# A ring of attention keys gets a copy of its first unit behind its end

## The chip, the cores and the metric

The kernel runs on one core of a Trainium2 chip. The metric is the device time of one execution in microseconds (us); a lower time is better. The profile is of one execution, recorded by the hardware profiler.

## What is computed

One encoder layer over 4096 tokens of 1024 channels. Two head groups run side by side: windowed attention (8 query heads of 64 channels, 2 key/value heads, each query sees keys at most 128 tokens away) and a pooling group. The part that the change touches is the product of queries and keys. Cut down, the reference says:

```python
kw = jnp.concatenate([kp[:, :-2], kp[:, 1:-1], kp[:, 2:]], axis=2)   # 3 blocks of 128 keys
s = jnp.einsum('bnqkgd,bnskd->bnkgqs', qb, kw).astype(jnp.float32) * scale
s = jnp.where(valid[None, :, None, None], s + bias[None, None], NEG)
m = jnp.maximum(jnp.max(s, axis=-1, keepdims=True), sk)
p = jnp.exp(s - m)
p = p / (jnp.sum(p, axis=-1, keepdims=True) + jnp.exp(sk - m))
o = jnp.einsum('bnkgqs,bnskd->bnqkgd', p.astype(v.dtype), vw)
```

Here `n` is a block of 128 queries; its keys are the block before, the block itself and the block behind it.

## The kernel before

The kernel has two stages. The first one, until some 500 us, norms the input, multiplies it by the gate and pooling weights and leaves what the second stage reads in DRAM. The second stage does the attention, the output projection and the closing norm. It walks over units of 256 tokens (two blocks each), from the first token to the last; units and blocks are numbered backwards in the code, and `ru(u)` and `rb(b)` turn a number into its place in the order of the tokens. "Block 7" below is the place in the order of the tokens.

Numbers are kept as pairs of float16 (a high part and a rest), so that every product is three products: high by high, rest by high, high by rest. The keys of a unit are projected by `proj_k` into PSUM, from which ScalarE writes the high part (`keep_k`) and VectorE the rest (`rest_k`) into `k_all`. That tile holds 2 x 1024 columns (high and rest): a ring of four units, in which a unit's place is its token number modulo 1024. Keys of both key heads lie in it, one in the upper and one in the lower 64 partitions.

`scores` is one visit of a block for half of its query heads. For the inner blocks it works in four parts of 32 queries, each against the 288 keys that these can see, for two heads in the two halves of the array at once (`gg`) and two PSUM tiles (`jj`): 2 x 3 x 4 x 2 = 48 matmuls of 32 x 288. The first two blocks and the last one take 128 queries at once, 12 matmuls. Where a part's 288 keys go over the end of the ring, the loop over `(lo, cut, k0), (cut, hi, 0)` makes two matmuls of it, one up to the ring's end and one from its beginning. That is the case for all four parts of blocks 7, 8, 15, 16, 23 and 24.

After a visit comes its softmax: VectorE adds the bias and takes the maximum (`logits`), ScalarE does the exponentials, VectorE and ScalarE make the probabilities as float16 pairs (`probs`, `rests`), and SP issues a transposing DMA into `pt_all` (`turn`). `values` multiplies them by the values of the unit later on.

The order on every engine is written out by hand: each step is put on a list by `due` with a planned time, `pe` and `visit` advance the plan's clock for TensorE, `settled` moves some steps on the other engines out of the softmax's way, and in the end the list is sorted by time and issued under a manual schedule. A plan time thus sets an order only; how long something takes is up to the engines. One turn of the loop over `m` covers two units (four blocks, eight visits). In it lie also three kinds of matmuls that the prediction names by their code: `q_product` (the queries of four units by a scheme with few products, from slots that `load_x` fills; "p3" reads the slot "Z"), `do_kv` (keys and values of a unit), and `product` (the output projection; its inputs are made by `high` on ScalarE and `low` on GpSimd). GpSimd also multiplies by the closing norm's gain (`gain`) and issues the DMAs of `add_x`. SP issues all other loads, stores and transposes in one queue.

Of the kernel before, what the change touches and what calls it, by code (L numbers as in the profile page):

```python
# [9 lines left out]
F16 = mybir.dt.float16  # L10
# [7 lines left out]
P = 128  # L18
# [33 lines left out]
UT = 2 * P  # L52
# [19 lines left out]
def hybrid_layer(ctx: ExitStack, tc, io, out):  # L72
    nc = tc.nc
# [81 lines left out]
    with ExitStack() as actx:  # L155
# [25 lines left out]
        def due(t, fn, *args):  # L181
            plan.append((t, len(plan), fn, args))
# [141 lines left out]
        gg = pa.tile([P, KT, P], BF16, name="gg", tag="yt")  # L324
# [861 lines left out]
        def tile0(si, t):  # L1186
            due(t, mm, si)
            after0(si, t + SLOT)
            return t + SLOT
# [10 lines left out]
        t = tile0(1, 29.3)  # L1200
# [8 lines left out]
        t = tile0(3, t + 1.9)  # L1209
# [9 lines left out]
        t = tile0(8, t + 4.2)  # L1219
# [4 lines left out]
        t = tile0(10, t)  # L1224
        t_last(1, t + 1.5)
        t = tile0(9, t)
# [6 lines left out]
        t = tile0(11, t)  # L1233
# [3 lines left out]
        t = tile0(4, t)  # L1237
        pair_split(5, t - 0.1)
        t = tile0(6, t)
        t_first(9, t + 5.5)  # L1240
        t_last(9, t + 10.0)
        t = tile0(5, t)
# [152 lines left out]
        for m in range(1, NM):  # L1395
# [7 lines left out]
            def op_at(i, z=z, step=step):  # L1403
                return z + i * step
# [13 lines left out]
            for i in range(7):  # L1418
                for c, q in enumerate(quads):
                    t = op_at(i) + c * PT  # L1420
# [8 lines left out]
    pb1 = ctx.enter_context(tc.tile_pool(name="pb1", bufs=1, reuse_waits="tile"))  # L1429
# [8 lines left out]
    wo[O12] = wo[OT4]  # L1438

    RK = 4 * UT  # L1440
    k_all = pb1.tile([P, 2, RK], F16, name="k_all")
    wq_b = pb1.tile([P, 3, 2, 2, HK, P], F16, name="wq_b")
    p_all = pb1.tile([P, 4, 3 * P], F32, name="p_all")
    q_t, v_t = {}, {}


    def rb(b):
        return NB - 1 - b

    def ru(u):  # L1450
        return NU - 1 - u
# [31 lines left out]
    def split_l(dst_h, dst_l, acc):  # L1483
        nc.vector.scalar_tensor_tensor(
            out=dst_l, in0=acc, scalar=QKV_EVAC, in1=dst_h, op0=ALU.mult, op1=ALU.subtract
        )
# [14 lines left out]
    def keys(b):  # L1501
        return [kb for kb in range(3) if 0 <= rb(b) - 1 + kb < NB]
# [10 lines left out]
    s_bank = [ps_s.tile([P, 2, 512], F32, name=f"s{i}") for i in range(2)]  # L1513

    def scores(b, half):
        u, tl = b // 2, rb(b) % 2 * P
        kbs = keys(b)
        first = (rb(b) - 1 + kbs[0]) * P
        if 0 < b < NB - 2:
            parts = [(QR * r, QR, QR * r, QR * r + NK) for r in range(P // QR)]  # L1520
        else:
            parts = [(0, P, 0, len(kbs) * P)]
        s_t[b, half] = s_bank
        for jj in range(2):
            for n, (qi, ki) in enumerate(((0, 0), (1, 0), (0, 1))):
                for r0, nr, lo, hi in parts:
                    k0 = (first + lo) % RK
                    cut = min(hi, lo + RK - k0)
                    for c0, c1, kc in ((lo, cut, k0), (cut, hi, 0)):
                        for gg in range(2 * (c1 > c0)):  # L1530
                            a = slice(64 * gg, 64 * gg + 64)
                            nc.tensor.matmul(  # L1532
                                s_bank[jj][r0 : r0 + nr, gg, c0:c1],
                                q_t[u, half][a, qi, jj, tl + r0 : tl + r0 + nr],
                                k_all[a, ki, kc : kc + c1 - c0], start=(n == 0 and c0 == lo),
                                stop=(n == 2 and c1 == hi), skip_group_check=True,
                            )

    def logits(b, half, i):

# [182 lines left out]
    def k_part(u, i):  # L1723
        ts = slice(ru(u) * UT % RK, ru(u) * UT % RK + UT)
        return k_all[:, i, ts]
# [6 lines left out]

    def rest_k(u):
        split_l(k_part(u, 0), k_part(u, 1), kv_t[u][:, 0])

    def keep_v(u):
        v_t[u] = pb.tile([P, 2, 2, P], F16, name=f"vv{u}", tag="v", bufs=3)
        split_h(v_t[u][:, 0], v_acc(u))
# [365 lines left out]
    def pe(us, fn, *args):  # L2104

        due(now[0], fn, *args)
        now[0] += us
        return now[0]
# [4 lines left out]
    def visit(b, half):  # L2113
        now[0] = max(now[0], free[0])
        t = max(pe(1.1, scores, b, half), free[1])
        softmax(b, half, t)
        free[:] = t + 2.9, t + 7.9

    def do_kv(u, i=2, late=0.0, k_high=0.0, k_low=0.5):
        pe(2.6, proj_k, u, i)  # L2120
        t = pe(2.8, proj_v, u)
        due(t - 2.8 + late + k_high, keep_k, u)
        due(t - 2.8 + late + k_low, rest_k, u)
        due(t + late, keep_v, u)
        due(t + 0.5 + late, rest_v, u)

# [75 lines left out]
    u = NU - 1  # L2202
# [8 lines left out]
    do_q(u, 0, 2)  # L2211
    due(now[0] - 2.0, lambda: nc.scalar.activation(dummy, mhalf, AF.Exp))
    do_kv(u, 0, 0.0, 0.2, 0.8)

    visit(NB - 1, 0)
    do_q(u, 1, 1)
    due(pe(2.6, q_product, 1, "p1", 0), q_keep, 1)
    due(now[0], load_x, 1, "Y")
    visit(NB - 1, 1)
    do_kv(u - 1, 2, 0.0, 0.7, 1.9)  # L2220
    visit(NB - 2, 0)
    turn_22(u, now[0] + 5.0)
# [7 lines left out]
    due(now[0], load_wq, 7, 2)  # L2230
    due(now[0] + 0.1, load_x, 1, "Z")
    do_kv(u - 2, 2)

    for m in range(1, NM):
# [25 lines left out]
        t = pe(M, q_product, m, "p2", 0, "p1")  # L2260
# [37 lines left out]
        t = pe(M, q_product, m, "p7", 1)  # L2298
# [10 lines left out]
        t = pe(M, q_product, m, "p4", 1, "p7")  # L2309
# [44 lines left out]
    at_(2.6, open_second, 2)  # L2354
    at_(2.6, product, 2, "s1", OT1, 1)
    at_(5.2, scores, 1, 0)
    at_(6.3, product, 1, "11", O11, 0)
    at_(8.9, product, 2, "s4", O22, 1, True)
    at_(11.5, values, 2)
    at_(13.6, scores, 1, 1)  # L2360
    at_(14.7, product, 1, "22", OT4, 2)
    at_(17.3, product, 1, "12", O21, 0, True)
# [161 lines left out]
```

## Time and profile before

| | |
|---|---|
| times of three runs | 1168.46, 1169.52, 1170.8 us (median 1169.52) |
| span of the profiled execution | 1163.3 us, first to last instruction (its own total time is not on the page) |
| TensorE busy (matmuls) | 1128.0 us, 97% |
| VectorE / ScalarE / GpSimd busy | 924.2 us, 79% / 758.0 us, 65% / 283.8 us, 24% |
| matmuls | 12528, of which 3432 score products |
| granted TensorE clock | 0.997 |
| DMA moved | 265.00 MB, mean 228 GB/s |

PE stands for TensorE, DVE for VectorE, ACT for ScalarE, POOL for GpSimd, SP and SPq for the SyncE queue that issues DMAs. In the timeline a row is: start, duration of the whole group, engine, line of the code, operation, what it writes and reads, shape, how many; in brackets the time that the engine idled before it and what ended that. In the table by stretches a row is: from and to, length, then busy time and number of instructions of PE, of PE's weight loads, of DVE, ACT and POOL, then granted clock, DMA share and GB/s. Matmuls overlap each other, so a step's cost on PE is read from its start to the start of the next step rather than from the duration of a row.

### The profile page before, as it was taken

How to read it: one execution, taken by the hardware profiler on the slowest of the kernel's cores; microseconds unless marked ns; L12 is line 12 of the kernel's file. 1: busy time of each engine (PE TensorE's matmuls, PEld its weight loads, DVE VectorE, ACT ScalarE, POOL GpSimd, SP SyncE). 2: the span in 40 equal slices, each digit the busy share in tenths (PEclk: the TensorE clock that was granted, in tenths of full speed). 3: DMA queues.
4: the chain of work that ended last, by engine and by line, in shares of the span. 5: the costliest groups of instructions: out<-in, count | busy, mean ns of one | idle time of the engine just before them, and what ended most of it. 6: DMA issues, size and time to landing. Idle time of an engine off the chain costs nothing.

```text
span 1163.3 us, 30484 instructions
## 1 busy us (share of the span) xinstructions
PE 1128.0 (97%) x12528; PEld 833.6 (72%) x12528; DVE 924.2 (79%) x1910; ACT 758.0 (65%) x1696; POOL 283.8 (24%) x270
## 2 busy tenths in 40 slices
PE   5999999999999999999999999999999999999997
PEld 4548888888888888887576676667666666766643
DVE  5788887778878886957887878878778778778896
ACT  5756666676465635166687767777677776777673
POOL 1000000000000000001454444454354444544322
PEclk9999999999999999999999999999999999999999
DMA  9577898696989856989799989899799899899877
GB/s 265 149 237 271 211 259 286 260 310 219 305 244 264 276 198 173 344 285 259 196 191 214 211 213 212 183 235 211 157 228 216 189 219 207 201 222 212 176 187 217
DMA packets 312635, 265.00 MB, mean 228 GB/s; under 512 B 214528, under 2 KB 275584, under 8 KB 303792
## 3 DMA queue, kind: packets, MB, share of 16 engines
q1 hardware_dynamic: 308464, 248.38, 78.1%
q0 software_dynamic: 4032, 14.68, 7.4%
q8 instruction: 98, 1.61, 0.5%
q14 instruction: 41, 0.34, 0.1%
HBM read 132.97 MB, written 79.21 MB: 182 GB/s over the span
## 4 chain that ended last, share of the span: by engine, by line
PE 45%; DVE 3%; DMA 3%; ACT 1%; issue 1%; SPq 0%; DVEq 0%; POOLq 0%; ACTq 0%
PE ms L2017 11%; PE aq_p L1754 9%; PE m L2017 8%; PE s L1532 4%; PE kv L1493 3%; PE kv L1716 3%; PE o L1870 3%; DMA pt_all<-pn 2%; PE z L1989 1%; PE o L1847 1%; DMA xt<-x_scr 1%; DVE pn L1605 1%; DVE p_all L1550 1%; PE ob L1847 1%; PE s L1989 0%
## 5 line engine op out<-in xcount | busy, mean ns | idle before, releaser
L990 PEld LDWEIGHTS <-wa 128*128 128x128 f16 x3360 | 329.7, 98 | 43.5 <-issue 4.8
L990 PE MATMUL ch<-xt,wa 128*128 128x256 f16 x1920 | 214.5, 274 | 2.6 <-ACT cbig L1002 1.7
L1561 ACT ACTIVATE p_all<-p_all,nm 128x384 f32<-128x384 f32 (+1 forms) x256 | 152.4, 596 | 41.3 <-DVE nm L1550 41.3
L1605 DVE SCALAR_TENSOR_TENSOR pn<-p_all,rd,pn 128x384 f16<-128x384 f32 (+1 forms) x256 | 144.5, 624 | 36.9 <-ACT pn L1597 36.1
L2017 PE MATMUL ms<-wo,ys 128*128 128x512 f16 x720 | 165.4, 379 | 2.9 <-DVE ys L1923 0.9
L1597 ACT ACTIVATE pn<-p_all,rd 128x384 f16<-128x384 f32 (+1 forms) x256 | 134.7, 597 | 36.6 <-DVE rd L1583 17.6
L1550 DVE CUSTOM_DVE_ANT_0 p_all<-s,ybig,nsink 128x384 f32<-128x384 f32 (+1 forms) x256 | 155.6, 663 | 1.7 <-PE s L1532 1.7
L2017 PEld LDWEIGHTS <-ys 128*128 128x128 f16 x720 | 68.8, 98 | 83.9 <-issue 2.5
L2017 PE MATMUL m<-wo,y 128*128 128x512 f16 x540 | 124.0, 379 | 1.4 <-DVE mo L2059 1.3
L990 PE MATMUL cl<-xt,wa 128*128 128x256 f16 x960 | 106.7, 273 | 0.8 <-DVE cbig L1015 0.6
L1923 POOL TENSOR_TENSOR y<-yf,y 128x512 f16<-128x512 f32 x29 | 33.5, 1157 | 270.4 <-DMA wo<-w_scr 158.9
L2017 PEld LDWEIGHTS <-y 128*128 128x128 f16 x540 | 51.6, 98 | 62.4 <-issue 2.5
L1754 PEld LDWEIGHTS <-raw 128*128 128x128 f16 x864 | 83.3, 98 | 18.0 <-issue 5.4
L211 POOL TENSOR_SCALAR ssq<-ssq 128x4 f32<-128x4 f32 (+1 forms) x11 | 3.6, 325 | 348.5 <-ACT jk L202 342.7
L1754 PE MATMUL aq_p<-xt,raw 128*128 128x256 f16 x672 | 77.9, 273 | 1.1 <-DVE nm L1550 1.1
L303 DVE TENSOR_TENSOR xt<-ybig,xt 128x1024 f16<-128x1024 f32 x56 | 67.2, 1219 | 13.0 <-ACT xt L298 11.4
L1923 POOL TENSOR_TENSOR ys<-at,ys 128x512 f16<-128x512 f32 x28 | 33.8, 1205 | 147.5 <-ACT ys L1919 123.9
L1532 PE MATMUL s<-k_all,q 64*32 64x288 f16 (+7 forms) x3432 | 63.1, 265 | 1.5 <-ACT k_all L1481 0.9
L1024 ACT ACTIVATE gp<-cbig,cg 128x256 f32<-128x256 f32 x42 | 19.0, 499 | 67.8 <-DVE cbig L1015 64.6
L2054 POOL TENSOR_TENSOR mo<-mo,ybig 128x512 f32<-128x512 f32 x39 | 51.4, 1317 | 44.2 <-ACT jkb L2043 43.9
L298 ACT CAST xt<-ybig 128x1024 f16<-128x1024 f32 x56 | 57.1, 1040 | 4.0 <-PE cl L990 2.1
L1754 PE MATMUL aq_p<-xt,wq_b 128*128 128x256 f16 x504 | 58.6, 273 | 0.0
(211 smaller groups left out, 1948.7 us busy)
## 6 DMA issues: line engine op xcount, KB each, us to landing
x_scr<-xt SPq DMA_DIRECT2D x16, 1024.0 KB
xt<-x_scr SPq DMA_DIRECT2D x16, 1024.0 KB
xn<-in_x SPq DMA_DIRECT2D x28, 512.0 KB
ybig<-in_xT SPq DMA_DIRECT2D x28, 512.0 KB
y_scr<-xt SPq DMA_DIRECT2D x14, 1024.0 KB
xt<-y_scr SPq DMA_DIRECT2D x14, 1024.0 KB
mo<-in_x POOLq DMA_DIRECT2D x28, 512.0 KB, 7.5
out<-mo SPq DMA_DIRECT2D x28, 512.0 KB
```

The costliest lines, as they stand in the source:

```text
L298: nc.scalar.copy(couple(m, c)[:, w, 0], y_view(i))
L303: eng.tensor_tensor(out=o[:, w, 1], in0=y_view(i), in1=o[:, w, 0], op=ALU.subtract)
L990: nc.tensor.matmul(acc[:, c], wa[:, q, wi, slot * HK + k, c * P : (c + 1) * P], x[:, xi, k, :], start=(fresh and n == 0), stop=(n > 3 * 2 ...
L1532: nc.tensor.matmul(s_bank[jj][r0 : r0 + nr, gg, c0:c1], q_t[u, half][a, qi, jj, tl + r0 : tl + r0 + nr], k_all[a, ki, kc : kc + c1 - c0], ...
L1550: nc.vector.tensor_tensor_reduce(out=p_t[b, half][:, hh, :nk], in0=s_t[b, half][jj][:, gg, :nk], in1=bias[:, h, lo : lo + nk], scale=negc[ ...
L1561: nc.scalar.activation(p[:, hh, :nk], p[:, hh, :nk], AF.Exp, bias=nm_t[b, half][:, hh : hh + 1], scale=-1.0, accum_out=den_t[b, half][:, h ...
L1597: nc.scalar.activation(prob_view(b, half)[:, 0, i], p_t[b, half][:, i, :nk], AF.Copy, scale=rd_t[b, half][:, 0, i : i + 1],)
L1605: nc.vector.scalar_tensor_tensor(out=pn4[:, 1, i], in0=p_t[b, half][:, i, :nk], scalar=rd_t[b, half][:, 0, i : i + 1], in1=pn4[:, 0, i], o ...
L1754: nc.tensor.matmul(acc[:, jj], w[:, wi, jj, k, :], x[:, xi, k, :], start=(first and n == 0), stop=(last and n > 3 * 2 * HK - 3), skip_grou ...
L1923: eng.tensor_tensor(out=y[:, :, 1], in0=f(u), in1=y[:, :, 0], op=ALU.subtract)
L2017: nc.tensor.matmul(z_t[u, tag], y[:, k, yi, :], wo[o][:, wi, k, :], start=(n == 0 and acc is None), stop=(n == 3 * HK - 1), skip_group_che ...
L2054: eng.tensor_tensor(out=mo, in0=mo, in1=gpost[:, cs], op=ALU.mult)
```

## The change

The tile of keys gets 256 columns more, behind the ring's end. When the keys of a unit are written that stands at the ring's first place (`ru(u) * UT % RK == 0`, from the second time on: the units at 1024, 2048 and 3072 tokens), GpSimd copies its high part and rest into these columns (`again_k`, 128 x 2 x 256 float16). `scores` then reads the keys of a part as one piece, which may run into the copy.

```diff
-    k_all = pb1.tile([P, 2, RK], F16, name="k_all")
+    k_all = pb1.tile([P, 2, RK + UT], F16, name="k_all")
...
-                    k0 = (first + lo) % RK
-                    cut = min(hi, lo + RK - k0)
-                    for c0, c1, kc in ((lo, cut, k0), (cut, hi, 0)):
-                        for gg in range(2 * (c1 > c0)):
-                            a = slice(64 * gg, 64 * gg + 64)
-                            nc.tensor.matmul(
-                                s_bank[jj][r0 : r0 + nr, gg, c0:c1],
-                                q_t[u, half][a, qi, jj, tl + r0 : tl + r0 + nr],
-                                k_all[a, ki, kc : kc + c1 - c0], start=(n == 0 and c0 == lo),
-                                stop=(n == 2 and c1 == hi), skip_group_check=True,
-                            )
+                    k0 = first % RK + lo
+                    for gg in range(2):
+                        a = slice(64 * gg, 64 * gg + 64)
+                        nc.tensor.matmul(
+                            s_bank[jj][r0 : r0 + nr, gg, lo:hi],
+                            q_t[u, half][a, qi, jj, tl + r0 : tl + r0 + nr],
+                            k_all[a, ki, k0 : k0 + hi - lo], start=(n == 0), stop=(n == 2),
+                            skip_group_check=True,
+                        )
...
+    def again_k(u):
+        if ru(u) and ru(u) * UT % RK == 0:
+            nc.gpsimd.tensor_copy(k_all[:, :, RK:], k_all[:, :, :UT])
...
+        due(t - 2.8 + late + k_low + 2.0, again_k, u)
```

On TensorE 576 matmuls and their weight loads go: 48 in each of 12 visits. In the first visit of block 7 (unit 12 by the code's number, PSUM tile s0) the rows before are these; each stands twice in the program, for the two head halves, and each with its own weight load:

```order
L1532 LDWEIGHTS q12_0_7889
L1532 MATMUL s0_5955<-k_all_5952,q12_0_7889 32x256
...
L1532 MATMUL s0_5955<-k_all_5952,q12_0_7889 32x32
...
L1532 MATMUL s0_5955<-k_all_5952,q12_0_7889 32x224
...
L1532 MATMUL s0_5955<-k_all_5952,q12_0_7889 32x64
...
L1532 MATMUL s0_5955<-k_all_5952,q12_0_7889 32x192
...
L1532 MATMUL s0_5955<-k_all_5952,q12_0_7889 32x96
...
L1532 MATMUL s0_5955<-k_all_5952,q12_0_7889 32x160
...
L1532 MATMUL s0_5955<-k_all_5952,q12_0_7889 32x128
```

At the same place, with the products ahead of the visit and behind it (p6 and p2 of the second turn), the rows now are:

```order
L1756 MATMUL aq2_p6_8272<-xt_72,wq_b_5953 128x256
L1530 LDWEIGHTS q12_0_7889
L1530 MATMUL s0_5955<-k_all_5952,q12_0_7889 32x288
...
L1530 MATMUL s1_5956<-k_all_5952,q12_0_7889 32x288
L1756 LDWEIGHTS raw_70
L1756 MATMUL aq2_p1_8227<-xt_72,raw_70 128x256
```

Each pair of pieces has become one matmul of 288 columns, in the same order, and what lies ahead and behind is unchanged. On GpSimd the end of the first turn of the loop, where the first of the three copies goes (`q` is the rest of a unit's queries, `y` the low part of "22" and then of "12", `mo` the output tile that `gain` multiplies, `rs` the norm's factor), stood so before:

```order
L1783 TENSOR_TENSOR q_0_7889<-kq_1_6216,q_0_7889 128x512
L1923 TENSOR_TENSOR y_13_7957<-yf_13_7637,y_13_7957 128x4x128
L2054 TENSOR_TENSOR mo_1_7974<-mo_1_7974,ybig 128x512
L1923 TENSOR_TENSOR y_13_8068<-yf_13_7816,y_13_8068 128x4x128
L2054 TENSOR_TENSOR mo_1_7974<-mo_1_7974,ybig 128x512
L2074 TENSOR_TENSOR rs_1_8103<-ms_1_8101,mhalf 128x1
```

and stands so now:

```order
L1785 TENSOR_TENSOR q_0_7889<-kq_1_6216,q_0_7889 128x512
L1925 TENSOR_TENSOR y_13_7957<-yf_13_7637,y_13_7957 128x4x128
L1736 COPY k_all<-k_all 128x2x256
L2056 TENSOR_TENSOR mo_1_7975<-mo_1_7975,ybig 128x512
L1925 TENSOR_TENSOR y_13_8069<-yf_13_7816,y_13_8069 128x4x128
L2056 TENSOR_TENSOR mo_1_7975<-mo_1_7975,ybig 128x512
```

The copy has come in between the low part of "22" and the gain; it waits for VectorE (the rest of the keys). The other two copies go to the same place of the third and fifth turn. The orders on VectorE, ScalarE and SP are the same as before.

## Prediction

> **What bounds the kernel now.** I read the page first, then the busy time in stretches of one macro block, then the PE engine's timeline, its waits, and last the queues behind the two waits that matter. The page gives the span, and says that PE's clock is granted in full:
>
> ```profile
> span 1163.3 us, 30484 instructions
> ...
> PEclk9999999999999999999999999999999999999999
> ```
>
> The second half of the program is a loop over pairs of units, and one turn is one macro block of the loop at the foot of the kernel. The five turns from m = 2 to m = 6, each cut at the start of its first score visit, stand so in the busy time by stretches (length, then PE busy):
>
> ```profile
> 615.13:697.00 81.87, 81.87 (x1202) 55.40 (x1202) 64.53 (x165) 59.33 (x149) 37.37 (x35) 1.00 0.93 208
> 697.00:777.86 80.86, 80.86 (x1010) 53.90 (x1010) 64.62 (x167) 59.45 (x149) 37.40 (x35) 1.00 0.95 206
> 777.86:861.15 83.29, 81.98 (x1201) 55.47 (x1201) 64.86 (x167) 59.52 (x149) 37.48 (x35) 1.00 0.91 208
> 861.15:942.01 80.86, 80.86 (x1009) 53.85 (x1009) 64.42 (x165) 59.42 (x149) 37.33 (x35) 1.00 0.89 208
> 942.01:1024.48 82.47, 81.94 (x1201) 55.39 (x1200) 64.79 (x167) 59.34 (x149) 37.45 (x35) 1.00 0.91 205
> ```
>
> The turns m = 3 and m = 5 are equal to the hundredth, 80.86 us, with PE busy from end to end. The turns m = 2, 4 and 6 hold some 190 matmuls more and last 1.01, 2.43 and 1.61 us longer; m = 2 has no idle time in it, so 1.01 us is what the extra matmuls cost PE. The other engines do the same in all five (DVE 64.4 to 64.9 us). So each stretch is set by PE, and the odd turns show what an even turn would be without cut key pieces.
>
> **The change part by part.** *The pieces.* A ring of 1024 key columns ends inside the window of blocks 7, 8, 15, 16, 23 and 24 (in the order of the tokens), each visited for two halves: 12 visits with 96 matmuls where the others have 48. The PE timeline has both kinds; the step from a visit's start to the start of the next product is what it costs:
>
> ```profile
> 716.41 0.93 PE L1532 MATMUL s<-k_all,q 64*32 64x288 f16 x48
> 717.27 2.79 PE L1754 MATMUL aq_p<-xt,raw 128*128 128x256 f16 x24
> ```
>
> ```profile
> 634.55 1.17 PE L1532 MATMUL s<-k_all,q 64*32 64x256 f16 x96
> 635.65 2.79 PE L1754 MATMUL aq_p<-xt,raw 128*128 128x256 f16 x24
> ...
> 993.04 1.19 PE L1532 MATMUL s<-k_all,q 64*32 64x128 f16 x96
> 994.16 2.79 PE L1493 MATMUL kv<-xt,raw 128*128 128x256 f16 x24
> ```
>
> A whole visit takes 0.86 us, a cut one 1.10 (blocks 7, 15, 23) or 1.12 us (blocks 8, 16, 24). The change makes all of the second kind into the first: 6 x 0.24 + 6 x 0.26 = 3.0 us of PE, which is also 3 x 1.01 from the stretches. All 12 visits lie where PE is busy before and behind them, so this is path time as long as nothing else ends last behind them.
>
> Here a rule speaks against so large a sum. The matmuls by shape are:
>
> ```profile
> L1532 PE MATMUL s<-k_all,q 64*32 64x96 f16 x144 | 12.1, 206 | 0.0
> L1532 PE MATMUL s<-k_all,q 64*32 64x64 f16 x144 | 11.9, 193 | 0.0
> L1532 PE MATMUL s<-k_all,q 64*32 64x32 f16 x144 | 11.6, 178 | 0.0
> ```
>
> One matmul gets 13 ns shorter from 96 to 64 columns and 15 ns shorter from 64 to 32: no floor between them, and both forms of a visit stream 288 columns for each term. The Trainium skill's page "TensorEngine Tiling (Array Packing)", section Instruction Overhead, says that a matmul has some 60 cycles of overhead and that one with a single column takes as long as one with 60. By that page only the 32-column pieces would cost anything: 28 columns too many, 6 times in a visit, at the 2.4 GHz of the Trainium skill's page "TensorE: Matmul & The Clock Gate" an estimated 0.07 us a visit and 0.8 us in all. The trace disagrees in both places: shapes show no floor there, and a cut visit is 0.24 us longer, so I keep 3.0.
>
> *What of it is lost.* Whether PE's time reaches the end is decided by the waits of PE from 560 us on:
>
> ```profile
> PE aq_p L1754 <- DVE nm L1550: 1.1, 1, 1.1
> ...
> PE o L1847 <- DMA pt_all<-pn: 0.7, 2, 0.5
> ```
>
> These two lie in the even turns. The rest of that list is ahead of the cut visits or behind 1118 us, where PE waits for softmax and gating steps that its own earlier work sets off, so they move along with it. The two are:
>
> ```profile
> 810.74 2.78 PE L1754 MATMUL aq_p<-xt,raw 128*128 128x256 f16 x24 [1.15 <-DVE nm L1550]
> ...
> 971.07 0.85 PE L1847 MATMUL o<-pt_all,vv 128*64 128x256 f16 x12 [0.53 <-DMA pt_all<-pn]
> ...
> 974.05 2.79 PE L1754 MATMUL aq_p<-xt,raw 128*128 128x256 f16 x24
> ```
>
> The 0.53 us at 971.07 is for the transposed probabilities of the visit before the first cut one, which SP issued here, while PE was in that cut visit:
>
> ```profile
> 961.78 4.03 SPq L1617 DMA_TRANSPOSE pt_all<-pn  x1
> ```
>
> So they land when they did, and PE, 0.24 us earlier, waits 0.24 us longer. The 1.15 us at 810.74 are laid to DVE, but the same product of the next even turn started at 974.05, and DVE reached the same instruction of its softmax only later:
>
> ```profile
> 974.17 0.67 DVE L1550 CUSTOM_DVE_ANT_0 p_all<-s,ybig,nsink 128x384 f32<-128x384 f32 x1
> ```
>
> So DVE is not what it needs. This product is p3, which reads the slot that load_x fills with "Z"; SP issued that load here, and in the odd turn ahead here:
>
> ```profile
> 710.59 0.39 SPq L1469 DMA_DIRECT2D xt<-y_scr  x1
> ...
> 790.87 0.39 SPq L1469 DMA_DIRECT2D xt<-y_scr  x1
> ```
>
> ```profile
> 727.95 2.79 PE L1754 MATMUL aq_p<-xt,raw 128*128 128x256 f16 x24
> ```
>
> In m = 3 it was there at the latest at 727.95, when p3 began without a wait, 17.4 us after its issue; in m = 4 PE got on after 19.9 us. That is a late load, and what the two cut visits ahead of it save (2 x 0.24) turns into waiting. So 3.0 less 0.24 less 0.48 gives 2.3 us if both waits stand as in this execution, 3.0 if neither does. The runs differ by 2.3 us among themselves, more than both waits together (1.68), so I can't tell how often they come; I take the middle, 2.65 us.
>
> *The copy.* Three times GpSimd copies 128 x 2 x 256 numbers, behind the rest of the keys of the units at 1024, 2048 and 3072 tokens. No copy of this kind is in the trace. Around the first place GpSimd and DVE do:
>
> ```profile
> 614.49 1.16 POOL L1923 TENSOR_TENSOR y<-yf,y 128x512 f16<-128x512 f32 x1 [5.56 <-ACT y L1919]
> 617.49 1.27 POOL L2054 TENSOR_TENSOR mo<-mo,ybig 128x512 f32<-128x512 f32 x1 [1.84 <-ACT jkb L2043]
> 620.49 1.16 POOL L1923 TENSOR_TENSOR y<-yf,y 128x512 f16<-128x512 f32 x1 [1.73 <-ACT y L1919]
> ```
>
> ```profile
> 613.07 0.42 DVE L1484 SCALAR_TENSOR_TENSOR k_all<-kv,k_all 128x256 f16<-128x256 f32 x1 [1.17 <-ACT k_all L1481]
> ```
>
> The keys are whole at 613.49, before GpSimd ends its low part at 615.65; it then sits idle for 1.84 us until ScalarE has squared. As many elements with two inputs take 1.16 us, so the copy is put at 0 to 1.3 us (the 1.27 of the row behind it at most) and lies in that gap; I take 1.16, the nearest row, and 0 on the path. The new wait for DVE has only the gain and the low part of "12" queued behind it, and both wait for ScalarE longer. Its reader, the cut visit at 634.55, comes 18 us later. If the gap were gone, the low part of "12", made at 620.49, would be up to 1.3 us late, and the product that needs it starts here, 5 us behind its end:
>
> ```profile
> 626.61 2.76 PE L2017 MATMUL m<-wo,y 128*128 128x512 f16 x12
> ```
>
> So still nothing. One effect remains: GpSimd can hold DVE. A small DVE operation took 1.15 us and ended at 608.96, with GpSimd's tensor operation ending at 608.93:
>
> ```profile
> 607.81 1.15 DVE L1583 TENSOR_SCALAR rd<-rd 128x4 f32<-128x4 f32 x1
> ...
> 607.78 1.15 POOL L1783 TENSOR_TENSOR q<-kq,q 128x512 f16<-128x512 f32 x1 [0.24 <-ACT q L1779]
> ```
>
> The price of that is at most 3 x 1.16 = 3.5 us of DVE, and DVE has 16 us a turn to spare; until 617.5 it works on operands from PSUM. The Trainium skill's "GPSIMD Engine Reference" (section Specifications) says that its SBUF interfaces are shared with VectorE and contend with DVE instructions in a 2-port mode or with two SBUF inputs; the trace agrees with 1.15 us. I count 0, with 0 to 0.5 us for the range.
>
> *The sum.* The profiled span goes from 1163.3 to 1160.6 us. The median of the runs shown is 6.2 us over that span, whose execution has no time of its own on the page; I leave those 6.2 us as they are: 1169.52 - 2.65 = 1166.9 us, 0.23% less.
>
> **The rivals.** *The even turns become odd turns.* If the late transfers come from the extra PE time, all three turns shrink to 80.86 us: 1.01 + 2.43 + 1.61 = 5.05 us, 1164.5. For it: the odd turns have no wait. Against it: m = 2 is cut and has none either, and the late load of m = 4 was issued before its first cut visit. Chance 0.12.
>
> *The transfers take the gain back.* DMA engines are busy for 0.89 to 0.95 of each turn. If Z lands no sooner than p3 starts today, each even turn loses 0.48 (3.0 - 1.4 = 1.6 us, 1167.9); if the X load for kv behind the second block binds too, all of it (1169.5). Against it: in the odd turns both come in time with PE running at the new pace. Middle 1168.7, chance 0.21.
>
> *Slower: late loads multiply.* The place is p3's first weight load, or the transposes just ahead. PE's earlier pace moves the SP queue's transposes against the 1 MB loads, and a turn in which Z takes 19.9 instead of 17.4 us costs 1.15 us. Three such turns more give 1170.3 us (2.65 - 3.45), and from five it is over the bound (2.65 - 5.75: 1172.6). For it: one turn shows such a load, and one cause would reach all turns alike. Against it: the four other turns shown don't have it. Chance 0.10, of it 0.08 slower.
>
> *Number of pieces is not the cause.* If a visit at the ring's end is long for another reason, reading the copy is as long: 1169.5, or 1168.7 with the page's floor alone. The stretches speak against it. Chance 0.05.
>
> **How the numbers follow.** The forecast itself has 0.52, from 2.3 to 3.0 us. What a measurement can tell here is about 0.2%, 2.3 us; so 0.38 of this counts as faster and 0.14 as the same. With 0.12 from the first rival that is faster 0.50; the 0.14, the second and the last rival and 0.02 of the third give the same 0.42; slower 0.08. The range runs from 1165.0, where most of the first rival is in, to 1169.6, which takes in all of the second; outside lie the slower case and a few hundredths.
>
> **What would show it.** Right: all visits of inner blocks have 48 matmuls of 288 columns and 0.86 us; m = 2 lasts 80.9 us; each copy lies in GpSimd's gap behind the low part of "22". Wrong: a visit over 0.9 us, a turn m = 2 over 81.4 us, a DVE operation stretched beside a copy with PE waiting behind it, or waits of p3 and of the value products that grow by what the visits gave.

## The result, and the profile after

The changed kernel takes 1163.78 us (median of 5 runs, 1160.95 to 1165.25) against 1169.61 us before (5 runs of the same series): ratio 0.9947, 95% interval 0.9931 to 0.9964, 4 to 8 us faster. The direction was the forecast one, the size, 5.8 us, over twice the forecast 2.65 us, and the time lies 1.2 us under the range. Over all series of this study the changed kernel has 29 timed runs with a mean of 1163.4 us and the one before 129 with 1168.8: 5.3 us apart, standard error 0.35. So the question is not whether 5 us are luck, but where the part beyond PE's 3.0 us comes from.

The page of the changed kernel gives a shorter span and 1149 instructions less:

```profile
span 1159.2 us, 29335 instructions
...
PE 1123.2 (97%) x11952; PEld 828.6 (71%) x11952; DVE 923.8 (80%) x1910; ACT 757.9 (65%) x1696; POOL 287.1 (25%) x273
```

The score visits of blocks 7 and 8 on PE, with the step behind each, in the timeline:

```profile
633.66 0.93 PE L1530 MATMUL s<-k_all,q 64*32 64x288 f16 x48
634.52 2.79 PE L1756 MATMUL aq_p<-xt,raw 128*128 128x256 f16 x24
...
653.10 0.93 PE L1530 MATMUL s<-k_all,q 64*32 64x288 f16 x48
653.97 2.76 PE L2019 MATMUL ms<-wo,ys 128*128 128x512 f16 x12
```

They last 0.86 and 0.87 us, like any other visit. The copy lies on GpSimd where it was expected, shorter than the nearest row had it:

```profile
612.66 1.16 POOL L1925 TENSOR_TENSOR y<-yf,y 128x512 f16<-128x512 f32 x1 [4.30 <-ACT y L1921]
613.76 0.61 POOL L1736 COPY k_all<-k_all 128x512 f16<-128x512 f16 x1
615.63 1.27 POOL L2056 TENSOR_TENSOR mo<-mo,ybig 128x512 f32<-128x512 f32 x1 [1.27 <-ACT jkb L2045]
```

0.61 us, and 1.27 us of the idle gap are left behind it. The VectorE operations beside it were not stretched: two of line 2061 took 0.69 us each, and 3 us later one took 0.68. The turns m = 2 to m = 6 by stretches (length, then PE busy):

```profile
613.28:695.11 81.83, 80.93 (x1010) 53.97 (x1009) 64.49 (x165) 59.47 (x149) 37.97 (x36) 1.00 0.93 217
695.11:777.27 82.16, 81.03 (x1009) 53.77 (x1008) 64.60 (x167) 59.46 (x149) 37.43 (x35) 1.00 0.91 202
777.27:858.62 81.35, 81.00 (x1011) 53.80 (x1010) 64.77 (x167) 59.47 (x149) 38.02 (x36) 1.00 0.92 208
858.62:939.48 80.86, 80.86 (x1011) 53.81 (x1010) 64.47 (x165) 59.46 (x149) 37.42 (x35) 1.00 0.90 209
939.48:1020.34 80.86, 80.86 (x1011) 53.86 (x1010) 64.60 (x167) 59.46 (x149) 37.98 (x36) 1.00 0.91 211
```

Every turn now has some 1010 matmuls and 80.9 to 81.0 us of PE. But the waits have moved: m = 2, 3 and 4 hold some, m = 6 none, and the turn m = 3, which had no wait before, is 1.3 us longer, mostly by this one:

```profile
769.28 2.79 PE L1493 MATMUL kv<-xt,raw 128*128 128x256 f16 x24 [1.13 <-DVE den L1579]
```

This execution's own time is known, 1160.95 us: 1.75 us over its span. In every other run of the study that has both numbers the difference is 1.7 to 2.0 us too. The profiled execution of the kernel before, with its span of 1163.3 us, must thus have taken about 1165 us, less than any of the five runs shown beside it.

### The profile page after: what moved, and what is told of

Its sections match the earlier page's. It is cut to its first block, busy times and chain, and to the rows that moved or that the text cites. A ratio compares the mean times of both kernels' runs of the same rounds, so it can differ in the third digit from the quotient of the medians.

```text
span 1159.2 us, 29335 instructions
## 1 busy us (share of the span) xinstructions
PE 1123.2 (97%) x11952; PEld 828.6 (71%) x11952; DVE 923.8 (80%) x1910; ACT 757.9 (65%) x1696; POOL 287.1 (25%) x273
## 4 chain that ended last, share of the span: by engine, by line
PE 61%; DVE 13%; DMA 11%; issue 5%; ACT 4%; SPq 1%; POOL 1%; DVEq 0%; POOLq 0%; ACTq 0%
PE ms L2019 12%; PE aq_p L1756 10%; PE m L2019 9%; PE ch L990 5%; PE s L1530 4%; DMA rs_scr<-ssq 3%; PE kv L1493 3%; PE kv L1714 3%; PE a L940 3%; PE cl L990 3%; DVE ws L855 3%; PE o L1872 3%; DMA xn<-in_x 2%; DVE xt L303 2%; DMA pt_all<-pn 2%
## 5 line engine op out<-in xcount | busy, mean ns | idle before, releaser
L1530 PE MATMUL s<-k_all,q 64*32 64x288 f16 (+2 forms) x2856 | 60.1, 284 | 1.5 <-ACT k_all L1481 0.9
```

The lines of the kernel that those rows point to most:

```text
L1530: nc.tensor.matmul(s_bank[jj][r0 : r0 + nr, gg, lo:hi], q_t[u, half][a, qi, jj, tl + r0 : tl + r0 + nr], k_all[a, ki, k0 : k0 + hi - lo], ...
```

## The experiments

My theory after the result: the cut pieces cost PE time and nothing else, so the gain is 3.0 us of PE, and the rest is how waits for transfers fell. The rivals: waits multiply PE time; the larger tile moves other tiles in memory; the number of instructions counts.

### Which part of the change does it

The changed kernel once more, unaltered.

> The changed kernel, unaltered, once more. PE time alone (the saving is the 3.0 us of the cut pieces, and the measured 5.8 us held some luck with the waits for transfers): 3 us below before, within 1 us. Every other theory (amplified waits, moved tiles, fewer instructions): again 5 to 6 us below.

1163.47 us, ratio 0.9955 (0.9940 to 0.9970): 5 us below before, so the first result was not a lucky draw.

The pieces alone, from the kernel before:

```diff
-                    k0 = (first + lo) % RK
-                    cut = min(hi, lo + RK - k0)
-                    for c0, c1, kc in ((lo, cut, k0), (cut, hi, 0)):
...
+                    k0 = min((first + lo) % RK, RK - (hi - lo))
+                    for gg in range(2):
```

> Whole pieces without the larger tile and without the copies: a window that would run over the ring's end is moved back to end at it, so those 12 visits read some wrong keys. PE time alone: 3.0 us below before. Cut visits amplified by waits: 5.8 below, as the changed kernel. Moved tiles (the 1 KB that the tile of keys gained changes where other tiles lie): 3.0 below, half of the gain missing. Fewer instructions: 5.8 below.

1163.26 us, ratio 0.9955 (0.9941 to 0.9969): the whole gain.

The tile and the copies alone, from the changed kernel:

```diff
-                    k0 = first % RK + lo
-                    for gg in range(2):
...
+                    k0 = (first + lo) % RK
+                    cut = min(hi, lo + RK - k0)
+                    for c0, c1, kc in ((lo, cut, k0), (cut, hi, 0)):
```

> The larger tile and the three copies, with the keys still read in two pieces. PE time alone, amplified waits, fewer instructions: same as before within 0.5 us. Moved tiles: some 2.8 us below before, the half of the gain that PE's time does not explain.

1167.85 us, ratio 1.0000 (0.9983 to 1.0018): nothing. The theory of moved tiles falls, and the copies cost nothing that can be measured.

PE time put back in another form:

```diff
-            for n, (qi, ki) in enumerate(((0, 0), (1, 0), (0, 1))):
+            terms = ((0, 0), (1, 0), (0, 1))
+            twice = len(parts) > 1 and rb(b) % 8 in (7, 0)
+            for n, (qi, ki) in enumerate(((0, 0),) * twice + terms):
...
-                            k_all[a, ki, k0 : k0 + hi - lo], start=(n == 0), stop=(n == 2),
+                            k_all[a, ki, k0 : k0 + hi - lo], start=(n <= twice), stop=(n == 2 + twice),
```

> The changed kernel, but in the 12 visits that were cut the first of the three products is done twice (16 matmuls of 288 columns more instead of 48 pieces, about the same 0.24 us on PE). PE time alone and amplified waits: same as before within 1 us. Moved tiles: 2.8 us below before. Fewer instructions (what counts is their number, 16 in place of 48): some 2 to 4 us below before.

Such a visit has 64 matmuls and takes 1.10 us, as a cut one had; here that of block 7 in the timeline of this run:

```profile
640.57 1.17 PE L1532 MATMUL s<-k_all,q 64*32 64x288 f16 x64
641.67 2.79 PE L1758 MATMUL aq_p<-xt,raw 128*128 128x256 f16 x24
```

1167.64 us, ratio 0.9997 (0.9980 to 1.0015): all of the gain is gone again, with a third of the instructions added. The number of instructions is not what counts; PE's time in these visits is.

### Does PE's time count once, more or less?

The keys of all 58 visits of inner blocks in two pieces, from the changed kernel:

```diff
+                    cut = lo + 160 if len(parts) > 1 else hi
+                    for c0, c1 in ((lo, cut), (cut, hi)):
...
+                                k_all[a, ki, k0 + c0 - lo : k0 + c1 - lo],
+                                start=(n == 0 and c0 == lo), stop=(n == 2 and c1 == hi),
```

> The changed kernel with the keys of all 58 visits of inner blocks read in two pieces (160 and 128 columns), 46 visits more than before. PE time alone, one for one: 46 x 0.26 = 12 us slower than before. Waits add to PE time in the measure of 5.2 to 3.0: some 20 us slower. Transfers set part of the pace, so that later PE time falls into their waits: 9 us or less.

1179.64 us, ratio 1.0096 (1.0066 to 1.0126): 11 us slower than before. A cut visit of this run takes 1.10 us, so PE's share is 46 x 0.24 = 11 us: one for one, within the interval (8 to 15 us).

The double product in all of them (`twice = len(parts) > 1`):

> The changed kernel with the first of the three products done twice in all 58 visits of inner blocks: the same 0.24 us of PE time a visit, by 16 matmuls instead of 48 pieces. PE time alone: 46 x 0.24 = 11 us slower than before, as with all keys cut. Waits add in the measure of 5.2 to 3.0: some 19 us. Were it the number of instructions: a third of what all keys cut costs.

1175.52 us, ratio 1.0062 (1.0041 to 1.0083), 5 to 10 us slower than before: PE's 11 us lie just outside that interval. With so much work on PE, one wait was left between 600 and 1110 us, where the executions of the kernel before hold 2.8 to 3.9 us of waits:

```profile
PE o L1851 <- DMA pt_all<-pn: 0.8, 1, 0.8
```

Both runs give the visits the same PE time, and yet the one with all keys cut is 4 us slower. Its waits of PE in the same window are:

```profile
PE aq_p L1759 <- issue: 1.6, 1, 1.6
PE s L1532 <- issue: 0.7, 1, 0.7
PE ms L2022 <- issue: 0.4, 1, 0.4
PE kv L1493 <- issue: 0.3, 1, 0.3
```

"issue" is time in which the engine waited for nothing that the profile shows. This run has the most matmuls of all, 14736 against 12880 with the double product, and no other profiled execution has more than 0.2 us of such stops in this window. So the extra matmuls cost more here than the visits' own time, and the "one for one" above is partly luck: these stops, 3.0 us, stand in the place of the waits for transfers. What PE stopped for is not shown.

The double product in 12 visits elsewhere (`twice = len(parts) > 1 and rb(b) % 8 in (3, 4) and rb(b) < 24`):

> The changed kernel with that double product in 12 visits of the first, third and fifth turn (blocks 3, 4, 11, 12, 19, 20) instead of those that were cut. PE time alone, wherever it lies: 3 us slower than the changed kernel, 2 below before. The place matters (the visits at the ring's end stand where a late PE meets late transfers): as in the double product at the ring's end, 4 to 5 us slower than the changed kernel there, but here only 3 or less.

1166.46 us, ratio 0.9990 (0.9973 to 1.0007): some 4 us above the changed kernel by the ratios, each to its own series (0.9990 and 0.9955). That lies between the two forecasts, and the interval, from 3.2 us below before to 0.8 above it, does not tell this place from the ring's end. Inconclusive.

The third of the three products left out, from the changed kernel:

```diff
+            terms = ((0, 0), (1, 0), (0, 1))[: 2 if len(parts) > 1 else 3]
+            for n, (qi, ki) in enumerate(terms):
```

> The changed kernel with the third of the three products (high part of the queries by the rest of the keys) left out in all 58 visits of inner blocks: 0.24 us of PE less in each, 14 us in all. PE time alone: 14 us below the changed kernel, 19 below before. Transfers close to the bound: PE waits for them instead, and 6 us or less of the 14 come out; the loop's turns then stay near 79 us with waits for loads and transposes in every one.

1154.04 us, ratio 0.9877 (0.9844 to 0.9910): some 9 us below the changed kernel (1163.47 in another series) for 14 us of PE. That is neither all of it nor the 6 us or less of the other expectation. Between 600 and 1110 us PE now waits above all for:

```profile
PE kv L1493 <- DMA xt<-x_scr: 3.0, 2, 1.5
PE o L1850 <- DMA pt_all<-pn: 2.1, 4, 1.1
PE o L1873 <- DMA pt_all<-pn: 0.9, 1, 0.9
```

So waits do not multiply PE time. Seen from the changed kernel they take back some of what PE gives up, and shrink where PE is slower. By this the 12 visits should be worth 3 us or less.

### The waits taken away

Half of the transposing DMAs, in the kernel before and in the changed one:

```diff
-        nc.sync.dma_start(t4, pn_t[b, half][:, : 8 * len(kbs) * P], transpose=True)
+        n = 4 * len(kbs)
+        nc.sync.dma_start(t4[:, :n], pn_t[b, half][:, : n * P], transpose=True)
...
-                        p[rows, pi, g, :, :, kb, (lo, hi)[side]],
+                        p[rows, 0, g, :, :, kb, (lo, hi)[side]],
...
-                            pt[b, half][:, pi, g, :, i, :], start=(n == 0), stop=(n == last),
+                            pt[b, half][:, 0, g, :, i, :], start=(n == 0), stop=(n == last),
```

> The kernel before with half of its transposes: only the high parts of the probabilities are turned, and the value products read them in place of the rests too (the same matmuls on PE; the rests' share of the sum is wrong). With its partner below it splits the 5.1 us into PE time and waits. If what goes beyond PE's 3.0 us lies in waits for transfers, those waits go here: no wait for the transposes is left in the loop, turns m = 2, 4 and 6 last 81.9 us, m = 3 and 5 80.9, and the time is 3 to 6 us below before, with less spread between runs. If it lies elsewhere, this kernel keeps it.

> The changed kernel with the same half of the transposes. Excess in waits for transfers: 3.0 us (within 0.7) below its partner with cut keys, all turns from m = 2 to m = 6 at 80.9 us. Excess elsewhere: 5 us below its partner.

The turns m = 2 to 6 with cut keys:

```profile
616.26:698.13 81.87, 81.87 (x1201) 55.38 (x1200) 64.54 (x165) 59.34 (x149) 37.36 (x35) 1.00 0.72 166
698.13:779.00 80.87, 80.87 (x1011) 53.92 (x1010) 64.62 (x167) 59.46 (x149) 37.43 (x35) 1.00 0.75 174
779.00:860.86 81.86, 81.86 (x1201) 55.38 (x1200) 64.82 (x167) 59.35 (x149) 37.42 (x35) 1.00 0.68 167
860.86:941.72 80.86, 80.86 (x1009) 53.80 (x1008) 64.48 (x165) 59.45 (x149) 37.35 (x35) 1.00 0.72 169
941.72:1023.60 81.88, 81.88 (x1202) 55.41 (x1202) 64.81 (x167) 59.35 (x149) 37.47 (x35) 1.00 0.74 170
```

and three of them with whole keys (the two left out read the same):

```profile
613.93:694.79 80.86, 80.86 (x1009) 53.88 (x1008) 64.49 (x165) 59.45 (x149) 37.93 (x36) 1.00 0.69 170
...
775.65:856.51 80.86, 80.86 (x1009) 53.87 (x1008) 64.60 (x167) 59.45 (x149) 37.95 (x36) 1.00 0.72 170
...
937.37:1018.23 80.86, 80.86 (x1009) 53.79 (x1008) 64.61 (x167) 59.45 (x149) 37.95 (x36) 1.00 0.74 171
```

With the DMA share down from 0.9 to 0.7, no wait is left in any of these turns, in either kernel, the one at p3 included: DVE does the same work in the same order here, so that wait comes with the transfers, as I had read it, and not from DVE, to which the profile lays it; whether with the load of "Z" or another transfer is not shown. The five turns hold 407.34 us with cut keys and 404.30 with whole ones: 3.04 us, PE's time exactly. From the first score visit to the end the two executions differ by no more than these 3.0 us; the first stage ended at 502.53 us in the one and at 500.19 in the other. The timed runs have 1164.30 us (ratio to before 0.9961, 0.9943 to 0.9979) and 1159.86 us (0.9928, 0.9910 to 0.9946), 4.4 us apart by the medians, more than 3.0 once more; the means (8 and 6 runs) are 4.4 apart with a standard error of 0.9, which does not exclude 3.0. The runs of this pair spread by 6.0 and 4.7 us, not less than others did. If their other executions are like the profiled ones, that spread lies in the first stage.

### More profiled executions

Unaltered kernels, for their traces.

> The kernel before, unaltered, for a second profiled execution of it. Waits by chance of the execution: the turns m = 3 and 5 at 80.9 us or a little more, m = 2, 4 and 6 at 81.9 us and over, with waits for transfers in other places than in the first profile. Waits fixed by the kernel: the same 1.1 us at the product p3 of m = 4 and 0.5 us at the value products of m = 6.

> The changed kernel, unaltered, for one more profiled execution. The turns m = 2 to 7 are explained (3.0 us of PE, waits of some 3 us in both kernels). The rest of the 5.1 us lies ahead of the first cut visit: if it is chance of the execution, the first stage here ends anywhere from 499 to 505 us, as in the kernel before, and the first turn lasts 77.2 to 78.7 us in both; if it comes with the change, the first stage ends 1 us sooner on average than in the two looks at the kernel before, and the first turn is 77.4 us here and 78.6 there.

> The kernel before, unaltered: partner of the look above. Chance: the first stage ends anywhere from 499 to 505 us, first turn 77.2 to 78.7 us. Tied to the kernel: first turn 78.6 us with the wait of 1.0 us at its second key projection.

> A second look at the changed kernel. Tied to the kernel: first turn 77.4 us, waits of 1 us at the second key projection of m = 3, none at m = 6. Chance: these waits in other places.

> A second partner. Tied to the kernel: first turn 78.6 us, waits of 1.1 us at p3 of m = 4 and 0.4 to 0.6 us at the value products of m = 6. Chance: these waits in other places.

Before: 1168.50 us (ratio 0.9995, 0.9979 to 1.0012), 1169.36 (1.0002, 0.9985 to 1.0020) and 1169.74 (1.0013, 0.9996 to 1.0030). Changed: 1163.75 us (0.9953, 0.9934 to 0.9972) and 1163.29 (0.9957, 0.9938 to 0.9975). With these there are four profiled executions of each kernel. Means in us, cut at the starts of score visits; a minus is a gain:

| stretch | before | changed | difference |
|---|---|---|---|
| first stage, to the first score visit | 502.61 | 501.43 | -1.19 |
| from there to m = 1 | 36.65 | 36.59 | -0.06 |
| m = 1 | 78.62 | 77.67 | -0.95 |
| m = 2 (cut before) | 82.50 | 82.17 | -0.33 |
| m = 3 | 80.86 | 81.92 | +1.06 |
| m = 4 (cut before) | 83.27 | 81.06 | -2.21 |
| m = 5 | 80.86 | 80.86 | 0.00 |
| m = 6 (cut before) | 82.32 | 81.02 | -1.30 |
| m = 7 and the tail | 138.80 | 138.84 | +0.04 |
| span | 1166.50 | 1161.55 | -4.95 |

The waits of PE between 600 and 1110 us in the last profiled execution of the kernel before, and in one of the changed kernel:

```profile
PE o L1847 <- DMA pt_all<-pn: 1.6, 3, 1.0
PE aq_p L1754 <- DVE nm L1550: 1.2, 1, 1.2
PE kv L1493 <- DMA xt<-x_scr: 1.1, 1, 1.1
```

```profile
PE o L1849 <- DMA pt_all<-pn: 2.2, 3, 1.0
```

The kernel before waited at p3 of m = 4 in all four executions (1.15, 1.07, 0.65 and 1.20 us), the changed kernel in none of its four; it waits in m = 3 instead, where the kernel before never did. The first turn lasts 78.6 to 78.7 us in all four before, 77.2 to 77.4 in three of the changed kernel, and 78.7 in the fourth. The wait that makes the difference stands in the first execution of the kernel before and in that fourth one of the changed kernel:

```profile
607.14 2.79 PE L1493 MATMUL kv<-xt,raw 128*128 128x256 f16 x24 [0.99 <-DMA xt<-x_scr]
...
607.19 2.79 PE L1493 MATMUL kv<-xt,raw 128*128 128x256 f16 x24 [1.08 <-DMA xt<-x_scr]
```

So the waits of the middle turns are nearly fixed by the kernel, and that of m = 1 is not: it comes in one execution of the changed kernel and not in the others. Nor does it go with the cut keys: the first turn lasts 77.4 us with the tile and the copies alone, whose keys are cut, and 78.7 with the double product at the ring's end, whose keys are whole. The first stage ends at 499.96, 502.39, 504.88 and 503.22 us before and at 499.33, 503.03, 503.45 and 499.89 us in the changed kernel: both have early and late ones.

One stop in the first stage does set the executions apart. In the first one of the kernel before, and at the same place in that of the changed kernel, PE does:

```profile
377.81 2.67 PE L990 MATMUL ch<-xt,wa 128*128 128x256 f16 x23
381.25 4.59 PE L990 MATMUL ch<-xt,wa 128*128 128x256 f16 x40 [0.77 <-issue]
```

```profile
377.80 7.26 PE L990 MATMUL ch<-xt,wa 128*128 128x256 f16 x65
```

All four executions of the kernel before stop there, for 0.77, 0.48, 1.42 and 0.72 us, and none of the changed kernel's four does. But the pieces alone, in one profiled execution, stop there too (0.93 us), and the tile and the copies alone do not, so the stop does not go with the gain.

## Why the prediction was wrong

**What held.** PE bounds the loop. The sum of the pieces, 3.0 us, was right to 0.04 us (the light pair). The copies and the larger tile cost nothing, and GpSimd had the gap for them; the 1.16 us taken for a copy were 0.61. The visits became equal, as the first point of "What would show it" had it. But m = 2 did not come down to 80.9 us: it lasted 81.83 to 82.57 us in the four executions, over the 81.4 that the prediction names as a sign of being wrong.

**First failed step: what is lost to waits.** I held that the late load of m = 4 and the transposes of m = 6, where they come, take 0.72 us of the 3.0, and put half of that into the sum. Both went: in m = 4 the changed kernel has no wait at p3 at all, and in m = 6 three executions of four have none. In their place m = 3 waits 1.1 us, and m = 2 more than before. Over m = 2 to 6 the waits come to 2.5 us before (409.81 less 407.33 of PE) and 2.7 us after (407.03 less 404.30). So the transfers took nothing to speak of: 2.8 of the 3.0 us came out here. My mistake was to hold a transfer's landing time fixed while its surroundings moved: with DMA engines busy nine tenths of the time, a turn m = 2 that gives PE 1 us less work changes which transfer of the turns behind it is late. That this is how they moved is my reading; shown is that the waits go with the transfers' load (the light pair) and that their sum stayed. The rival that the even turns become odd turns is nearly right for m = 4 and m = 6 and wrong for m = 2 and m = 3, which hold the waits now; that its 1164.5 us lies nearest to the measured time is luck, since of its 5.05 us in these turns 2.8 came out. It is luck, too, that the forecast's 2.65 us were close to these 2.8.

**Second failed step, the one that put the time out of the range: nothing was counted ahead of the first cut visit.** The prediction sets aside whatever "is ahead of the cut visits", the wait for a load at 607.14 in m = 1 with it, and it read no row of the first stage. In the means of four executions 2.2 of the 4.95 us lie there: 1.19 in the first stage and 0.95 in m = 1, where that wait is gone in three executions of four. Over all timed runs the gain is 5.3 us, and the first series drew 0.5 us more than that (5.8). The 1169.52 us that the sum starts from was met (1169.61), so the starting point is not what failed. But the 6.2 us "over that span" were misread: what lies around a span is 1.75 us, and the other 4.5 say that the execution profiled was an early one (first stage done at 499.96 us, against 502.4 to 504.9 in three others). The difference between executions, which lies mostly in the first stage, thus had no view at all.

**What is open.** The timed runs give 5.3 us (standard error 0.35), the loop from m = 2 on 2.8. The rest, 2.2 us in the spans of four executions each, lies ahead of the first visit that was cut: 1.2 us in the first stage, nearly all else in the first turn. Neither the tile and the copies (1.0000) nor, by the double product at the ring's end (1167.64), the number of instructions alone can be made answerable, and it comes back in full with PE time in these visits. In the four executions each it looks like chance: early and late first stages occur in both kernels, the wait of the first turn in both. The one stop that only the kernel before has, at line 990, makes 0.85 us of it on average, but the pieces alone have both that stop and the whole gain. And 29 against 129 runs are too many for chance in the total. I have no mechanism by which score visits after 630 us act on work before 615 us, and no experiment here isolates one. What the experiments settle is which edit does it (the pieces, by PE's time), and that 3.0 us of it are PE's time one for one (the light pair). The cause of the rest stays open.

**The rivals.** That transfers take the gain back was the second likeliest, and the run with two products shows it to be real some way further on (9 us out of 14), not in these 3 us. Late loads did not multiply. That the number of pieces is not the cause is refuted twice: whole pieces bring the gain, and in the all-cut run pieces of 128 and 160 columns, with no short one among them, cost 0.24 us a visit as well.

## What to carry to other kernels

An operand that wraps around costs the matmuls that it cuts, even where the streamed columns stay the same, and a copy of the ring's first part on an engine with idle time was a cheap way out here. Read what cut and whole forms cost from their start-to-start steps in the same trace, and compare turns of a loop that differ in nothing else: both gave 3.0 us before any run. Do not take a wait as fixed because it is there in every execution of one kernel: here such waits vanished and others came as soon as PE's work ahead of them changed. And read several executions of a kernel, the stages that a change does not touch included, before setting a narrow range.

## What the runs showed of the hardware that was not expected

A visit cut into pieces of 160 and 128 columns takes as long as one with pieces of 32 to 256. From the timeline of the run with all keys cut:

```profile
704.49 1.17 PE L1532 MATMUL s<-k_all,q 64*32 64x160 f16 x96
705.59 2.76 PE L2022 MATMUL ms<-wo,ys 128*128 128x512 f16 x12
```

1.10 us, 0.24 more than whole, for 48 matmuls and their weight loads more: 5 ns for each, in both cuts. The Trainium skill's page "TensorEngine Tiling (Array Packing)", section Instruction Overhead, says that each matmul has some 60 cycles of overhead and that one with a single column takes as long as one with 60. Read as a floor under short matmuls, as in the prediction, that would charge nothing here: no piece is under 128 columns, and the measured cost is that of the cut with short pieces.

A one-input float16 copy of 512 elements a partition took 0.61 us on GpSimd, a two-input operation of as many elements, from float32 to float16, 1.16 us.

The same kernel spreads by some 10 us within one series (1164.09 to 1173.76 us in 31 runs before). The end of its first stage moved by 4.9 us between four profiled executions.
